# A hybrid trunk layer in split fp32: gate tiles spread over six delta heads, the attention branch moved beside the last two, state products in column strips

## Chip, cores and metric

The kernel runs on one core of one Trainium2 chip. The metric is device microseconds of one execution, here the median of three runs. Times inside the kernel come from one profiled execution, counted from its first instruction.

## What is computed

One layer of a decoder for 1024 prompt tokens and 8 single sample tokens (together NT = 1032 columns), width 1024. In short:

```
h   = RMSNorm(x) * (1 + scale1) + shift1
z   = h @ w_in            # q|k|v of the delta rule, its gate, beta, decay, q, k, v of attention, ga, gb
y_a = W_a( GatedRMSNorm( GatedDeltaRule( conv4(q, k, v) ) ) )
y_b = W_b( SlidingWindowSinkAttention(q, k, v) )
x   = x + gate1 * W_o( sigmoid(ga) * y_a + sigmoid(gb) * y_b )
x   = x + gate2 * W_down( silu(conv3(h2 @ W_gate)) * (h2 @ W_up) ),  h2 from x as h
```

The delta rule has 8 heads of 128 x 128 states. The prompt runs in eight chunks of 128 from a zero state. Each of the 8 samples has a carried state S per head and makes one step: S is scaled by exp(g), delta = (v - k S) * beta, then S + k delta, and q S is the output. All new states are outputs.

## The kernel before, in words

**Products.** Activations lie transposed: 128 channels in the partitions, tokens in columns, in eight channel blocks. Every fp32 operand is split into a high and a low half (`split`, L125: the high half on ScalarE, the difference on VectorE), and a product is three matmuls (`mm3`, L176). `project_steps` (L150) makes one output tile of 128 channels; the columns come in three *token parts* (`PARTS`: 384, 384 and 264 columns), each with 8 steps of 3 matmuls into one PSUM bank. A weight tile is 1024 x 128, 512 KB. `load_w` (L138) loads it on SyncE's DMA queue into a raw buffer and splits it into wh and wl. `where` names the pool: the main pool wp has two wh/wl pairs and one raw buffer, the side pool pg one of each.

**Order.** The order in the program isn't the order of issue. Each instruction has a priority from where the program stands (`cur_priority`), and a planner with a simulated timeline puts each engine's instructions in order: what is due first goes first, and what has a far priority goes where its engine would idle. `weave` (L1225) gives each stream of work a start and a step in that numbering; `issue_after` ties an instruction behind another. Once planned, each engine's order is fixed.

**Stages around the change.**

- Attention (up to about 435 us) leaves its output in DRAM (`ob`, 8 x 128 x 1032).
- Delta heads 0 to 7 (`run`, L1918). For each head h the streams are `unit_inverse` (L974, the inverse of a unit triangular 128 x 128 matrix from blocks of 16, 32 and 64), `delta_scan` (L910, eight chunks in sequence, each a chain of small matmuls with VectorE and ScalarE between), `delta_prepare` for head h+1, and `head_projections` (L791): for heads 0 to 5 the gate tile of head h (`delta_gate`, L834) and the three convolved tiles of head h+2. The output of a head goes to DRAM (`oa`).
- The filler. `gates` (L1248) is a generator of 16 weight tiles, sigmoid of gb and ga, stored to DRAM as `sgb` and `sga`. Each `next` is one step of three matmuls, 24 to a tile. Two tiles are drawn in the attention. Heads 0 to 5 draw `pieces(3)`, three parts, at a priority 10000 behind (L1927); the last two heads draw 12 and 24 pieces as `head_projections`, with loads in turn into side and main pool.
- Branches (`branches`, L1271). `ob` is loaded and split, for all three token parts, into rooms of its own. Then for each of 8 output tiles the weight `w_swa_out` is loaded once and multiplied with all three parts; the result times `sgb` stays in SBUF (`ub`). Between the parts stand the steps of `sample_delta` (L1095), the samples' delta rule, whose states and temporaries lie in the room of h (`b1`). Its products k S and q S (L1147) have a stationary operand of 16 columns and give 16 PSUM partitions. Its state stores go out on SyncE's queue, its output into the last 8 columns of `oa`. With the last two tiles `oa` is loaded and split. Then comes the product with `w_gdn_out`: times `sga`, plus `ub`, split into `mix`, which takes the room of `b1`.
- The second half (L1829): w_o, the second norm and the feed-forward part. The change doesn't touch it.

Names in profile lines: `b1h,wh` are products with h (projections and gate tiles), `b2h,wh` those of the branches; `rc`, `o` belong to the scan; `tp` to the inverse and preparation; `gt` is a gate tile's staging buffer; `raw` a raw weight buffer.

Of the kernel before, what the change touches and what calls it, by code (L numbers as in the profile page):

```python
# [9 lines left out]
F32 = mybir.dt.float32  # L10
# [8 lines left out]
P = 128  # L19
NP = 1024  # L20
NS = 8
# [41 lines left out]
class Step:  # L63
# [358 lines left out]
    def attention(self, pool, psum):  # L422
# [10 lines left out]
        self.filler, self.fill_where, self.gt = self.gates(), [self.where], (pool, "mrows")  # L433
# [298 lines left out]
    def delta_setup(self):  # L732
        nc = self.nc
        self.oa = self.t(self.dr, [8, P, NT], "oa")
# [43 lines left out]
    def delta_project(self, pa, pool, h):  # L778

        K = self.t(pool, [P, NCH, P], "K", bufs=3)  # L780
        Q = self.t(pool, [P, NCH, P], "Q", bufs=3)
        V = self.t(pool, [P, NCH, P], "v0", bufs=1)
# [51 lines left out]
    def delta_gate(self, pa, pool, h):  # L834

        nc = self.nc
        sg = self.t(pool, [P, NT], "sg", bufs=1)
# [9 lines left out]
        self.sg = sg  # L847
# [62 lines left out]
    def delta_scan(self, pool, psum, h, prep):  # L910
        nc, sg = self.nc, self.sg
# [183 lines left out]
    def sample_delta(self):  # L1095
# [3 lines left out]
        a, b, c, d, e = (self.t(self.b1, [P, KC, PARTS[t][1]], f"b1{x}{t}", F32R).bitcast(F32).rearrange("p k n -> p (k n)")  # L1099
                         for x, t in (("h", 1), ("l", 1), ("h", 2), ("l", 2), ("h", 0)))  # L1100
        small = carver(d, e)
        S0 = []
        for h in range(H):
            S0.append((a, b, c)[h // 3][:, h % 3 * NP:h % 3 * NP + NP].rearrange("p (b v) -> p b v", b=NS))
            nc.sync.dma_start(S0[h], I["state_gdn_S"][0][:, h].rearrange("b k v -> k b v"))
        act, tmp = small(24, NS), small(24, NS)
# [11 lines left out]
        wide = small(H, NS, 2 * NS)  # L1118
        nc.gpsimd.memset(wide, 0.0)
        yield  # L1120
        ps = self.t(self.psm, [P, 1], "mm")
# [12 lines left out]
        dots = self.t(self.psm, [P, H, NS], "mm")  # L1134
# [7 lines left out]
        rows = small(H, P, r=1)[:2 * NS]  # L1142
        for h0 in (0, 4):
            ps = self.t(self.psm, [2 * NS, 4, P], "mm")
            for h in range(4):
                for b in range(NS):
                    nc.tensor.matmul(ps[:, h, :], wide[:, h0 + h, b, :], S0[h0 + h][:, b, :], start=b == 0, stop=b == NS - 1)  # L1147
            nc.scalar.copy(rows[:, h0:h0 + 4, :], ps)
            yield
        pks = self.t(self.psm, [P, H, NS, 2], "mm")  # L1150
        for h in range(H):
            self.transpose(pks[:, h].rearrange("p b a -> p (b a)"), rows[:, h, :])
# [7 lines left out]
        ps = self.t(self.psm, [H * NS, P], "mm")  # L1160
        self.transpose(ps, f3(dl))
        dlT = small(P, r=1)[:H * NS]
# [9 lines left out]
        ps = self.t(self.psm, [H * NS, 1], "mm")  # L1172
# [5 lines left out]
        nc.vector.scalar_tensor_tensor(o, o, self.onw, self.sgs, op0=ALU.mult, op1=ALU.mult)  # L1178
        nc.sync.dma_start(self.oa[:, :, NP:NT].rearrange("i p b -> p i b"), o)

        for h in range(H):
            if h % 4 == 0:
                yield
            db = self.t(self.b1, [P, KC, 384], "b1l0", F32R).bitcast(F32).rearrange("p k n -> p (k n)") if h == 0 else db
            d = db[:, h % 3 * NP:h % 3 * NP + NP].rearrange("p (b v) -> p b v", b=NS)
            nc.sync.dma_start(d, dlr[h].unsqueeze(0).broadcast_to([P, NS, P]))
            nc.gpsimd.tensor_tensor(d, d, bc(kq[:, h, :, 0], 2, P), op=ALU.mult)
            for b in range(NS):
                nc.vector.scalar_tensor_tensor(S0[h][:, b, :], S0[h][:, b, :], self.egb[:, b, 0, h:h + 1], d[:, b, :],
                                               op0=ALU.mult, op1=ALU.add)  # L1190
            nc.sync.dma_start(self.O[3][0][:, h].rearrange("b k v -> k b v"), S0[h])

    def rows_rsqrt(self, small, ps, n, scale, eps):

        nc = self.nc
        r = small(2, r=1)
        nc.vector.tensor_scalar(r[:n, 0:1], ps, scale, eps, op0=ALU.mult, op1=ALU.add)
        self.power(r[:n, 1:2], r[:n, 0:1], self.mhalf)
        dg = small(P, r=1)
# [71 lines left out]
    def branches(self, pool, pool2):  # L1271
# [4 lines left out]
        for _ in self.filler:  # L1276
            pass
# [710 lines left out]
```

## Time and profile before

| what | value |
|---|---|
| median of 3 runs (lowest, highest) | 2168.84 us (2162.29, 2172.43) |
| the profiled execution | 2160.1 us, its span 2158.3 us |
| granted TensorE clock, mean | 0.976 |
| first state copy of the scans of heads 0 to 7 | 533, 616, 701, 779, 855, 930, 1007, 1093 us |
| last product with h (end of the gate tiles) | 1146.7 us |
| attention branch (`w_swa_out` products) | 1146.6 to about 1260 us |
| delta branch (`w_gdn_out` products) | about 1260 to 1350 us |

How to read the views: in the table of stages each row is a stretch, its length, then the busy time of each engine with its instructions in it, the granted TensorE clock (PEclk, 1.00 is full), the mean busy share of 16 DMA engines (it can go over 1, since overlapping packets are summed) and GB/s. PE is matmul, PEld weight load. A list of waits has who waited, for whom, the total, the number and the longest. A line of the timeline has start, duration, engine, line, operation, output and inputs, shape, count, and in brackets the idle time before it and what ended it. Matmuls are pipelined, so their durations overlap: what one costs is the distance between starts.

### The profile page before, as it was taken

Reading aid. Unit: us, or ns where it says so; the run is one execution under the profiler, and the core shown is the slowest. Engines: PE = TensorE matmul, PEld = TensorE weight load, DVE = VectorE, ACT = ScalarE, POOL = GpSimd, SP = SyncE. Lnnn points to the kernel's source line nnn. Section 1 sums busy time; section 2 is a strip of 40 time slices with the busy share of each in tenths; the row PEclk is TensorE's granted clock in tenths of the full one; section 3 lists DMA queues with packets and bytes.
Section 4 is the critical chain, followed back from the end, with each engine's and each line's share of the span. In section 5 each row is a group of like instructions: output and inputs, shape, how many; then the busy total and the mean of one; then the engine's idle time right before and its main releaser. Section 6 shows DMA issues by size and latency. Waiting matters only on the chain. (4 is left out here: it accounts for less than half of the span.)

```text
span 2158.3 us, 41369 instructions
## 1 busy us (share of the span) xinstructions
PE 2075.7 (96%) x16309; PEld 1957.4 (91%) x16309; DVE 1384.7 (64%) x2781; ACT 849.8 (39%) x2118; POOL 520.4 (24%) x583
## 2 busy tenths in 40 slices
PE   7999998999899999999999999999999999999998
PEld 4985887899899988998999999898999999999998
DVE  4756667374555756765323565468888788778876
ACT  3655446334234334344332032344333343444533
POOL 1000000020221110211111200002655655645631
PEclk8999999999999999999999999999999999999999
DMA  8256432151321321221318663612232323378962
GB/s 278 77 139 200 154 139 89 41 143 42 84 83 55 78 58 40 63 66 46 95 45 245 189 207 102 190 52 72 89 118 94 108 94 96 120 267 285 325 227 82
DMA packets 298981, 268.68 MB, mean 124 GB/s; under 512 B 60558, under 2 KB 246321, under 8 KB 298770
## 3 DMA queue, kind: packets, MB, share of 16 engines
q1 hardware_dynamic: 294450, 250.39, 37.3%
q0 software_dynamic: 4048, 15.12, 2.0%
q8 instruction: 128, 2.10, 0.4%
q14 instruction: 67, 0.55, 0.1%
q10 hardware_dynamic: 288, 0.52, 0.1%
HBM read 207.29 MB, written 61.07 MB: 124 GB/s over the span
## 5 line engine op out<-in xcount | busy, mean ns | idle before, releaser
L178 PE MATMUL mm<-b1h,wh 128*128 128x384 f32 (+1 forms) x1392 | 457.2, 329 | 4.5 <-ACT z L764 2.1
L180 PE MATMUL mm<-b1h,wl 128*128 128x384 f32 (+1 forms) x1392 | 452.2, 325 | 3.6 <-DVE wl L128 3.6
L179 PE MATMUL mm<-b1l,wh 128*128 128x384 f32 (+1 forms) x1392 | 450.0, 323 | 0.0
L178 PEld LDWEIGHTS mm<-b1h,wh 128*128 128x128 f32 x1392 | 263.6, 190 | 14.2 <-issue 4.7
L180 PEld LDWEIGHTS mm<-b1h,wl 128*128 128x128 f32 x1392 | 263.4, 189 | 10.1 <-issue 5.5
L179 PEld LDWEIGHTS mm<-b1l,wh 128*128 128x128 f32 x1392 | 263.6, 189 | 3.1 <-issue 2.8
L127 ACT ACTIVATE wh<-raw 128x1024 fp32r<-128x1024 f32 x75 | 78.7, 1049 | 158.3 <-PE mm L179 80.3
L128 DVE TENSOR_TENSOR wl<-raw,wh 128x1024 fp32r<-128x1024 f32 x74 | 90.7, 1225 | 66.5 <-ACT wh L127 65.8
L179 PE MATMUL mm<-pk,w 128*128 128x260 f32 (+1 forms) x440 | 124.9, 284 | 0.8 <-DVE pk L128 0.8
L178 PE MATMUL mm<-pk,w 128*128 128x260 f32 (+1 forms) x440 | 124.9, 284 | 0.6 <-ACT pk L127 0.6
L178 PE MATMUL mm<-b2h,wh 128*128 128x384 f32 (+1 forms) x384 | 123.4, 322 | 1.7 <-ACT wh L127 1.7
L180 PE MATMUL mm<-pk,w 128*128 128x260 f32 (+1 forms) x440 | 124.7, 284 | 0.0
L179 PE MATMUL mm<-b2l,wh 128*128 128x384 f32 (+1 forms) x384 | 122.7, 320 | 0.0
L180 PE MATMUL mm<-b2h,wl 128*128 128x384 f32 (+1 forms) x384 | 121.9, 320 | 0.6 <-DVE wl L128 0.6
L128 DVE TENSOR_TENSOR w<-ws,w 128x512 fp32r<-128x512 f32 x88 | 74.3, 846 | 37.7 <-ACT w L127 37.7
L1563 ACT COPY bml<-mm 128x256 f32<-128x256 f32 (+1 forms) x132 | 49.3, 374 | 107.7 <-PE mm L180 100.9
L178 PE MATMUL mm<-bmh,w 128*128 128x260 f32 (+1 forms) x320 | 90.7, 283 | 0.1
L180 PE MATMUL mm<-bmh,w 128*128 128x260 f32 (+1 forms) x320 | 90.5, 283 | 0.0
L179 PEld LDWEIGHTS mm<-pk,w 128*128 128x128 f32 x440 | 83.4, 189 | 1.0 <-DVE pk L128 1.0
L178 PEld LDWEIGHTS mm<-pk,w 128*128 128x128 f32 x440 | 83.4, 190 | 1.0 <-ACT pk L127 0.8
L180 PEld LDWEIGHTS mm<-pk,w 128*128 128x128 f32 x440 | 83.6, 190 | 0.0
L178 PEld LDWEIGHTS mm<-b2h,wh 128*128 128x128 f32 x384 | 72.7, 189 | 2.8 <-ACT wh L127 2.2
(632 smaller groups left out, 6081.5 us busy)
## 6 DMA issues: line engine op xcount, KB each, us to landing
raw<-in_w_in_dram SPq DMA_DIRECT2D x60, 512.0 KB
ws<-in_w_ffn_down_dram SPq DMA_DIRECT2D x55, 256.0 KB
raw<-xd SPq DMA_DIRECT2D x47, 258.0 KB
raw<-in_w_ffn_down_dram SPq DMA_DIRECT2D x47, 256.0 KB
raw<-in_w_ffn_gate_dram SPq DMA_DIRECT2D x22, 512.0 KB
raw<-in_w_ffn_up_dram SPq DMA_DIRECT2D x22, 512.0 KB
qst<-in_w_mod_dram SPq DMA_DIRECT2D x16, 512.0 KB
raw<-in_w_mod_dram SPq DMA_DIRECT2D x16, 512.0 KB
```

Of the source, the lines that this page charges most:

```text
L127: self.nc.scalar.activation(hi, x, AF.Copy)
L128: (eng or self.nc.vector).tensor_tensor(lo, x, hi.bitcast(F32), op=ALU.subtract)
L178: mm(ps, whi, xhi, start=first, stop=False, **kw)
L179: mm(ps, whi, xlo, start=False, stop=False, **kw)
L180: self.last_mm = mm(ps, wlo, xhi, start=False, stop=last, **kw).ins
L1563: self.last_copy = nc.scalar.copy(r[p, i], x[p])
```

## The change

- The delta heads 0 to 5 draw `pieces(6)` instead of 3: twice the gate parts.
- Head 6 draws both last delta gates (of heads 6 and 7), so `sg` is kept for each head; the second lies in a z buffer.
- A new generator `early_out` follows the gates in the filler: the attention branch, by token part (0, 2, 1), 24 parts of one output tile each. The weight tile is loaded anew for each part (two parts ahead; of three loads two go to the main pool and one to the side pool). `ob` goes into the rooms of h as these come free; the gated product goes to DRAM (`ubd`) and is read back in `branches`.
- The samples' chain runs in it: five steps early, the rest from the 17th part on. Its temporaries lie in the buffers K, Q, v0 and th of the delta heads (K, Q and v0 now in a pool of their own, pk), its PSUM tiles in `pmf`, a single buffer. The products k S and q S go to four strips of 32 PSUM partitions, four heads side by side, and eight transposes become two. State stores go out on GpSimd's queue. The samples' output stays in SBUF (`osm`).
- `branches` keeps only the delta branch; parts 0 and 1 of `oa` are given the priorities of the 18th and 21st part of the new filler. PSUM has a pool of four further buffers there instead of two and two.

The diff, cut to its core:

```diff
-        self.filler, self.fill_where, self.gt = self.gates(), [self.where], (pool, "mrows")
+        self.filler, self.fill_where, self.gt = chain(self.gates(), self.early_out()), [self.where], (pool, "mrows")
...
-        sg = self.t(pool, [P, NT], "sg", bufs=1)
+        sg = self.t(pool, [P, NT], "sg", bufs=1) if h + 1 < H else self.t(pa, [P, NT + 3], "z")[:, :NT]
...
+        e, f, g = (self.t(self.pk, [P, NCH, P], tag).rearrange("p n i -> p (n i)") for tag in ("K", "Q", "v0"))
+        small = carver(e, f, self.t(self.pa, [P, 512], "th"), g)
...
-        rows = small(H, P, r=1)[:2 * NS]
-        for h0 in (0, 4):
-            ps = self.t(self.psm, [2 * NS, 4, P], "mm")
+        rows = small(2, P, r=3)
+        nc.gpsimd.memset(rows, 0.0)
+        for i in range(2):
+            if i:
+                c, d = room("h", 2), room("l", 2)
+                for h in (6, 7):
+                    load(h, c)
+            ps = self.t(self.pmf, [P, P], "mm")
+            for b in range(NS):
+                for h in range(4):
+                    nc.tensor.matmul(ps[32 * h:32 * h + 2 * NS], wide[:, 4 * i + h, b, :], S0[4 * i + h][:, b, :],
+                                     start=b == 0, stop=b == NS - 1)
             for h in range(4):
-                for b in range(NS):
-                    nc.tensor.matmul(ps[:, h, :], wide[:, h0 + h, b, :], S0[h0 + h][:, b, :], start=b == 0, stop=b == NS - 1)
-            nc.scalar.copy(rows[:, h0:h0 + 4, :], ps)
+                at = slice(32 * h, 32 * h + 2 * NS)
+                (nc.scalar.copy if h % 2 else nc.vector.tensor_copy)(rows[at, i, :], ps[at])
             yield
...
-        nc.sync.dma_start(self.oa[:, :, NP:NT].rearrange("i p b -> p i b"), o)
...
-            nc.sync.dma_start(self.O[3][0][:, h].rearrange("b k v -> k b v"), S0[h])
+            nc.gpsimd.dma_start(self.O[3][0][:, h].rearrange("b k v -> k b v"), S0[h])
...
+    def early_out(self):
+        nc, order = self.nc, (0, 2, 1)
+        self.ubd = [self.t(self.dr, [8, P, n], f"ub{t}") for t, (_, n) in enumerate(PARTS)]
+        load = lambda i: self.load_w(self.I["w_swa_out"][0][:, i % 8 * P:(i % 8 + 1) * P],
+                                     where=self.fill_where[i % len(self.fill_where)])
+        X = {t: [self.part_room(self.b1, t, x, "b1") for x in "hl"] for t in (0, 2)}
+        self.load_part(self.ob, 0, *X[0])
+        samples = self.sample_delta()
+        ws, self.marks = [load(0), load(1)], []
...
+        g = gate(0)
+        for i in range(24):
+            t, j = order[i // 8], i % 8
+            self.marks.append(self.tc.cur_priority)
+            def out(t, ps):
+                nc.vector.tensor_tensor(s, ps, s, op=ALU.mult)
+                nc.sync.dma_start(self.ubd[t][j], s)
+            for k, _ in enumerate(self.project_steps(ws.pop(0), X, out, (t,), self.fill_psum)):
+                if k == 0:
+                    if i == 0:
+                        self.load_part(self.ob, 2, *X[2])
+                    if i == 8:
+                        X[1] = [self.part_room(self.b1, 0, x, "b1") for x in "hl"]
+                        self.load_part(self.ob, 1, *X[1])
+                    if i < 22:
+                        ws.append(load(i + 2))
+                    s, g = g, gate(i + 1) if i < 23 else None
+                if k in (2, 5) and (2 * i + k // 3 < 5 or i > 15):
+                    with self.tc.issue_after(self.last_mm):
+                        next(samples, None)
+                yield
...
-        ob = [self.load_part(pool2, self.ob, t) for t in range(3)]
+        here, oa = self.tc.cur_priority, []
+        for t, i in ((0, 17), (1, 20)):
+            self.tc.cur_priority = self.marks[i]
+            oa.append(self.load_part(self.oa, t, room[f"h{t}"], room[f"l{t}"]))
+        self.tc.cur_priority = here
+        oa.append(self.load_part(self.oa, 2, room["h2"], room["l2"], self.osm))
...
+        for t in range(3):
+            nc.sync.dma_start(ub[t], self.ubd[t].rearrange("j p n -> p j n"))
...
-        for j in range(6):
-            w = self.load_w(I["w_swa_out"][0][:, j * P:(j + 1) * P])
...
-                        self.fill_where, self.fill_psum = [self.fill_side, self.where], None
+                        self.fill_where, self.fill_psum = [self.where, self.fill_side, self.where], None
...
-                        streams.append((self.pieces(3), 10000, 100))
+                        streams.append((self.pieces(6), 10000, 100))
                     else:
-                        streams[1:1] = [(self.delta_gate(pa, pool, h), 500, 1)]
+                        if h + 2 == H:
+                            streams[1:1] = [(chain(*(self.delta_gate(pa, pool, i) for i in (h, h + 1))), 500, 1)]
                         streams.append((self.head_projections(pa, pool, h), 600, 100))
...
-            self.psm, more = self.pool("qs", 2, PSUM, ctx=c), self.pool("qb", 2, PSUM, ctx=c)
+            more = self.pool("qb", 4, PSUM, ctx=c)
```

111 lines of the change are left out of this document (54 added, 57 removed).

## The prediction, on record before the changed kernel ran

> **What bounds the kernel now.** First the head of the page, then the table of stages, with cuts at the first state copy of each delta head's scan (533, 616, 701, 1007, 1093), at the end of the gate tiles (1147) and at the start of the product of the delta branch (1260).
>
> ```profile
> span 2158.3 us, 41369 instructions
> PE 2075.7 (96%) x16309; PEld 1957.4 (91%) x16309; DVE 1384.7 (64%) x2781; ACT 849.8 (39%) x2118; POOL 520.4 (24%) x583
> ```
> ```profile
> core 0: us, PE busy (x) PEld busy (x) DVE busy (x) ACT busy (x) POOL busy (x), PEclk, DMA share, GB/s
> 533.00:616.00 83.00, 76.41 (x678) 72.22 (x677) 38.37 (x97) 29.12 (x96) 18.39 (x26) 0.96 0.28 78
> 616.00:701.00 85.00, 82.89 (x749) 79.97 (x747) 51.56 (x108) 30.70 (x85) 15.25 (x24) 1.00 0.24 64
> ...
> 701.00:1007.00 306.00, 288.91 (x2629) 275.64 (x2630) 197.89 (x438) 119.39 (x363) 47.20 (x74) 0.95 0.23 59
> ...
> 1007.00:1093.00 86.00, 84.38 (x749) 80.99 (x748) 32.86 (x93) 28.43 (x79) 16.35 (x24) 0.98 0.28 79
> 1093.00:1147.00 54.00, 53.97 (x363) 53.50 (x363) 14.96 (x29) 15.97 (x41) 10.22 (x15) 0.99 0.32 109
> 1147.00:1260.00 113.00, 109.28 (x723) 105.34 (x722) 57.26 (x132) 19.00 (x26) 21.30 (x13) 0.98 0.76 227
> 1260.00:1350.00 90.00, 89.71 (x574) 89.39 (x574) 52.08 (x108) 24.86 (x60) 0.00 (x0) 1.00 0.40 118
> ```
>
> TensorE bounds every stage, so moving a product gains nothing by itself; what can be gained is lost TensorE time. I count as lost the idle time (length minus PE busy) plus length times (1 minus PEclk). 701 to 1007: 17.1 idle + 306 x 0.05 = 15.3, together **32.4 us**. 616 to 701: 2.1. 533 to 616: 6.6 + 3.3 = 9.9. 1007 to 1147: 3.9. 1147 to 1260: 3.7 + 2.3 = **6.0**. After that nothing. Why the long stretch loses and the one before it doesn't, the stores of the gate tiles and the waits in that stretch say:
>
> ```profile
> L1263 SPq DMA_DIRECT2D sga<-gt x24: 319/320/1640, 1017.4 to 1165.2; - x24
> L1263 SPq DMA_DIRECT2D sgb<-gt x18: 319/335/580, 484.5 to 700.6; - x18
> L1263 SPq DMA_DIRECT2D sgb<-mrows x6: 319/320/320, 394.9 to 433.3; - x6
> ```
> ```profile
> PE tp L1058 <- ACT W L1049: 5.9, 4, 1.6
> PE rc L938 <- ACT s L936: 3.6, 7, 0.6
> PE rc L934 <- DVE y L932: 2.2, 4, 1.6
> PE rc L188 <- DVE vn L960: 2.1, 3, 0.7
> ```
>
> A gate tile is three parts, so three stores. Two tiles lie in the attention (x6), six (x18) between 484 and 701, eight (x24) from 1017. The filler of six heads is used up in the first three: from 701 to 1007 TensorE waits in the chain of the block inverse and the scan with nothing put between.
>
> **The change, part by part.** A tile of 8 x 3 parts x 3 products takes 90 / 8 = 11.25 us (row 1260: 8 tiles); by columns 4.2 us for a part of 384 and 2.9 us for the one of 264.
>
> *Twice the filler in six heads.* Six tiles, 67.5 us, leave the stretch behind 1007 and come ahead of it: no work gained or lost. The gain is lost time filled. The streams of 701 to 1007 are those of 616 to 701, where five parts brought the loss to 2.1; over 306 us at that rate it is 2.1 x 306/85 = 7.6, so 32.4 - 7.6 = **-24.8**. Supply: five parts in 85 us are 18 parts, six tiles, in 306 us, just what is added. The other end is 533 to 616, where four tiles stood with no projections and 9.9 was lost: 9.9 x 306/83 = 36.5, a loss of 4. I take -24.8, since the nearest row has the same streams.
>
> *Products with the sample states.*
>
> ```profile
> L1147 PE MATMUL mm<-b1h,b1l x80: 272/273/282, 1169.9 to 1188.2; 128*16 128x128 f32 x80
> L1147 PE MATMUL mm<-b1l,b1l x48: 272/273/282, 1175.1 to 1184.7; 128*16 128x128 f32 x48
> ```
> ```profile
> 175.61 1.07 PE L262 MATMUL mm<-wmh,cTr 128*32 128x512 f32 x2 [0.56 <-DMA wmh<-in_w_mod_dram]
> 175.62 1.07 PE L262 MATMUL mm<-wml,cTr 128*32 128x512 f32 x2
> 176.47 1.07 PE L262 MATMUL mm<-wmh,cTr 128*32 128x512 f32 x2
> ```
>
> 128 records between 1169.9 and 1188.5; a 4.4 us product tile lies between, so 14.3 us, 0.11 each. In four column strips four run side by side, as the modulation's do, whose starts in one group lie 0.01 us apart: 14.3 / 4 = 3.6, **-10.7**. Bounds: nothing (weight loads that don't overlap) and -10.7; the modulation is the only row of such strips, and it overlaps. Eight transposes become two; the eight small copies lie on ACT and DVE, which idle.
>
> *The attention branch as filler.* Its 24 parts (90 us) and the samples' chain move beside the last two heads, whose filler was the gates: cover is the same in kind, so their 3.9 stays, and the branch stage's 6.0 goes: **-6.0**. New is supply. The old order loaded a 512 KB weight tile for three parts, the new one for each part: 16 loads more, and 16 splits more on ACT (1.06) and DVE (1.22), 17 and 20 us that lie in idle time of both (row 1007). Two loads of three go through the one raw buffer of the main weight pool, which comes free after the DVE split:
>
> ```profile
> 1173.02 0.38 SPq L133 DMA_DIRECT2D raw<-in_w_swa_out_dram  x1
> ...
> 1179.61 0.38 SPq L133 DMA_DIRECT2D raw<-in_w_swa_out_dram  x1
> ```
> ```profile
> 1177.26 1.06 ACT L127 ACTIVATE wh<-raw 128x1024 fp32r<-128x1024 f32 x1 [5.64 <-DMA raw<-in_w_swa_out_dram]
> ```
> ```profile
> 1178.36 1.23 DVE L128 TENSOR_TENSOR wl<-raw,wh 128x1024 fp32r<-128x1024 f32 x1 [4.55 <-ACT wh L127]
> ```
> ```profile
> 1217.05 1.06 SPq L133 DMA_DIRECT2D raw<-in_w_swa_out_dram  x1
> ```
> ```profile
> 1224.29 1.06 ACT L127 ACTIVATE wh<-raw 128x1024 fp32r<-128x1024 f32 x1 [15.40 <-DMA raw<-in_w_swa_out_dram]
> ```
>
> From issue to issue one cycle is 6.6 us when DMA is quiet, and 7.2 + 1.1 + 1.2 = 9.5 when it isn't. Three parts need two cycles: 13.2 to 19. The parts of token part 0 lie beside the scan, which covers them. Token part 2 takes 8.7 per three: 4.5 short, 9 us over the six parts that come after the scan. Token part 1 takes 12.6: 0.6 to 6.4 short, 2 to 17 us over eight parts. Sum 11 to 26; I take 15, near the quiet cycle. Change from gate tiles to this filler: the rooms of h part 0 are refilled from DRAM, and TensorE has only the last tile's other two parts (7.1 us):
>
> ```profile
> L1217 SPq DMA_DIRECT2D b2l<-ob x12: 360/447/1361, 1136.7 to 1146.1; - x12
> ```
> ```profile
> 1145.07 0.85 ACT L127 ACTIVATE b2h<-b2l 128x768 fp32r<-128x768 f32 x1 [0.21 <-DMA b2l<-ob]
> ```
>
> First issue to fourth split was 1136.7 to 1145.9, 9.2 us, so 2 are left. Together **+17**.
>
> *Queues.* SP issues 16 loads, 24 stores of the gated products and 3 reads more, and 8 state stores and one of the samples' output less: 34 x 0.38 = 13 us over some 200 us; nothing, while SP doesn't wait. The state stores move to GpSimd's queue, behind its eight products per state; nobody waits there. Samples' temporaries now take the single spare PSUM buffer, which every third product tile also takes: nothing while evacuations keep pace, up to 5 if each of some ten steps makes a tile wait half a microsecond. The reads of the last token part come when two parts of the next product have run; seven PSUM buffers cover them.
>
> **Sum** against the profiled execution (span 2158.3, 2160.1 with what lies around it): -24.8 - 10.7 - 6.0 + 17 = **-24.5**, so 2136. The median shown is 2168.84, 8.7 above that execution; carried over, **2144**.
>
> **Rivals.** (a) *The loads are hidden*: the planner puts state steps and scan between, and the 17 is 0: -41.5, 2127. For it: DMA share is 0.28 and 0.32 in the last two heads; against: the single raw buffer.
>
> (b) *The gain is eaten*: -10 to +10, 2168. Either the filler is again used up early, in four heads instead of six (half of -24.8), with loads at 9.5; or stalls reach 40. For it: six heads' filler was gone after three.
>
> (c) *Slower: the attention branch becomes bound by DMA.* Its stretch moves 12.6 MB of weights, 4.2 each of attention output, states read, states stored, broadcast deltas, gates and gated products, and 6.2 of early reads for the next stage: 44 MB, in about 105 us of TensorE work (90 of parts, the rest scan and samples).
>
> ```profile
> 1210.00:1262.00 52.00, 47.99 (x291) 46.55 (x290) 38.32 (x89) 9.52 (x11) 14.38 (x8) 0.97 0.85 264
> ...
> 1146.00:1170.00 24.00, 24.00 (x159) 23.85 (x158) 11.97 (x26) 7.08 (x12) 5.50 (x4) 1.00 1.13 314
> 1218.00:1260.00 42.00, 38.92 (x237) 38.01 (x238) 28.32 (x75) 7.63 (x9) 10.22 (x5) 0.96 1.00 310
> ```
>
> At the 264 GB/s of the first row 44 MB take 167 us, +62 instead of +17: +20, **2189**. It decides below 300 GB/s (147 us, +42, which eats -41.5), if all 44 MB must land before the next stage. For it: the three rows are that traffic at a full DMA. Against: stores and early reads (10 MB) needn't land in it, and the other 34 MB take 110 us at 310.
>
> The Trainium skill speaks on this in "DMA: Bandwidth & Descriptors", section Specifications: HBM gives one core about 358 GB/s. By that limit the 44 MB would take 123 us, an estimate, +18, and (c) couldn't be slower. The rows saturate at 310 to 314 with 512-byte runs, so I don't lower its chance for it.
>
> The skill's page "TensorE: Matmul & The Clock Gate", section "Why this matters for your kernels", says the clock drops for TensorE idle gaps over about 3 us. The longest wait of the rows above is 1.6 us and yet PEclk is 0.95 in that stretch. By the rule filling would return idle time alone, 17.1 - 7.6 = 9.5 instead of 24.8, and the time would be 2160: it falls into (b), and as the rows speak against it I add nothing there.
>
> **How the numbers follow.** Forecast (2134 to 2157) 0.42, (a) 0.20, (b) 0.15, (c) 0.23. Faster by over 0.5% (10.8 us, about what a measurement of this kernel can tell from no change) is forecast and (a): 0.62; within: 0.15; slower: 0.23. The range goes from full filling without stalls (-49 with all of 32.4 returned, 2120) to (c): 2118 to 2188.
>
> **What would show it.** Right: gate stores spread to about 1000, PEclk 0.98 or more between 701 and the sixth head, the state products in about 4 us, first product of the delta branch some 20 us earlier, and TensorE waits of 10 to 20 us in all on the DVE split of weights or on a loaded weight. Wrong: gate stores that stop before 900; waits on weights over 40 us; DMA share at 1 over all of the branch; waits on GpSimd or the single PSUM buffer.

## The result, and the profile after

The changed kernel takes **2179.17 us** in the median (2174.00 to 2183.69 in 11 runs), the kernel before on the same chips 2169.91 (2162.07 to 2176.66 in 11): a ratio of **1.0044**, 95% interval 1.0026 to 1.0062, so 9.5 us slower by the ratio and 9.3 between the medians. 2144 was forecast; the range of 2118 to 2188 holds the time, the sign is wrong. All ratios use fast runs alone; the only slow one, 3399.34 us in the experiment on the operand reads, is left out.

The profiled execution has a span of 2172.3 us. Its table of stages is cut at the first state copies of the scans and, behind 1054, where the waits change:

```profile
700.00:788.00 88.00, 86.64 (x768) 84.10 (x767) 51.13 (x111) 32.10 (x97) 14.99 (x23) 1.00 0.27 71
788.00:882.00 94.00, 92.03 (x801) 90.12 (x802) 53.24 (x118) 35.85 (x111) 17.50 (x26) 0.98 0.26 68
882.00:967.00 85.00, 83.32 (x750) 80.36 (x749) 50.64 (x105) 30.49 (x84) 14.84 (x24) 1.00 0.24 64
967.00:1054.00 87.00, 82.87 (x748) 80.69 (x747) 53.89 (x118) 32.86 (x100) 14.20 (x21) 0.98 0.28 73
1054.00:1108.00 54.00, 52.29 (x466) 50.41 (x464) 30.56 (x85) 17.86 (x54) 11.59 (x18) 1.00 0.42 113
1108.00:1151.00 43.00, 37.72 (x342) 33.51 (x340) 18.64 (x36) 16.83 (x29) 2.31 (x3) 0.94 0.77 228
1151.00:1180.00 29.00, 25.17 (x161) 23.98 (x159) 14.21 (x27) 10.60 (x23) 1.59 (x1) 0.91 0.53 162
1180.00:1207.00 27.00, 24.79 (x185) 23.70 (x185) 12.99 (x22) 8.01 (x16) 2.40 (x3) 1.00 0.65 185
1207.00:1265.00 58.00, 43.20 (x266) 38.62 (x267) 32.38 (x69) 15.07 (x18) 12.59 (x10) 0.88 0.84 253
1265.00:1286.00 21.00, 19.52 (x110) 19.11 (x109) 10.16 (x24) 3.67 (x6) 5.41 (x4) 0.92 1.05 357
1286.00:1355.00 69.00, 68.04 (x441) 67.44 (x439) 47.67 (x117) 18.09 (x51) 5.74 (x4) 1.00 0.53 159
```

Lost time is counted as in the prediction, idle time plus length times (1 minus PEclk). The scans of heads 2 to 5 (700 to 1054) lose 12.8 us now, where 32.4 were lost. The scan of head 6 begins at 1053.6 instead of 1007.5, and this execution had begun its heads 2.8 earlier: 67.5 us of filler came in for 48.9, a gain of **18.6**. Behind it, 1054 to 1355, **44.2 us** are lost: 1.7, 7.9, 6.4, 2.2, 21.8, 3.2 and 1.0 row by row. Before, it was 3.9 + 6.0 + 0.3 = 10.2 from 1007 to 1350. The change put one hole in the place of another.

The ledger by first state copies, last evacuation of the delta branch (1350.4 before, 1354.5 after) and first product with w_o (1352.5, 1362.8):

| stretch | before | after | forecast | measured |
|---|---|---|---|---|
| to the first scan | 532.6 | 529.8 | 0 | -2.8 |
| scans 0 to 5, with 67.5 us more filler | 474.9 | 523.8 | -24.8 | -18.6 |
| from scan 6 to the last delta evacuation, with 67.5 less | 342.9 | 300.9 | +0.3 (-10.7 - 6.0 + 17) | +25.5 |
| to the first w_o product | 2.1 | 8.3 | 0 | +6.2 |
| from there to the end | 805.8 | 809.5 | 0 | +3.7 |
| span | 2158.3 | 2172.3 | -24.5 | +14.0 |

The gate stores show that the filler reaches as far as it was meant to: six of them, two tiles, lie behind the start of scan 6, and the last is at 1115. The products with the states run in two halves, the first from 1129.2 to 1131.1; of the second two start at 1216.0, and after a further wait for a state the rest runs from 1218.2 to 1221.4:

```profile
L1280 SPq DMA_DIRECT2D sga<-gt x24: 319/332/1703, 704.3 to 1115.2; - x24
```
```profile
L1157 PE MATMUL mm<-b1h,Q x80: 272/273/421, 1129.2 to 1221.2; 128*16 128x128 f32 x80
...
L1157 PE MATMUL mm<-b1l,Q x48: 272/385/421, 1129.2 to 1221.0; 128*16 128x128 f32 x48
```

The waits of TensorE from 1054 to 1365 (total, times, longest), then those of SyncE's queue from 1100 to 1290:

```profile
PE mm L1418 <- ACT w L127: 8.3, 1, 8.3
PE mm L180 <- DVE wl L128: 7.4, 8, 3.9
PE mm L178 <- ACT wh L127: 6.6, 8, 1.4
PE mm L1157 <- DMA b1h<-in_state_gdn_S_dram: 5.9, 2, 4.3
PE rc L934 <- DVE y L932: 2.3, 2, 1.5
PE mm L188 <- ACT th L1090: 2.0, 1, 2.0
```
```profile
SPq L1302 <- DMA ub<-gt: 24.5, 12, 5.7
SPq L1312 <- DVE gt L1311: 15.6, 10, 4.2
SPq L133 <- DVE wl L128: 7.2, 6, 2.4
```

TensorE waits 14.0 us for weight tiles, 5.9 for the states of heads 6 and 7, 8.3 for w_o. All the waits of that window, the short ones that are not shown too, come to 37.7 us, and the rows above add some 14 us of lowered clock from 1108 to 1286. SyncE's queue, which issues nearly every load, stands still for 113 us of 190: gate reads wait until a product store has left their buffer, stores wait for their product, and the loads of weights, states and operands stand behind them. That alone shows no cause, though: in the same 190 us of the kernel before, the queue stood still for 124, and TensorE lost little.

At w_o the order had turned round. SyncE's queue after, then before:

```profile
1348.95 7.53 SPq L1410 DMA_DIRECT2D x<-xT  x16
1356.58 3.76 SPq L1427 DMA_DIRECT2D raw<-in_w_o_dram  x3
```
```profile
1342.09 2.60 SPq L1383 DMA_DIRECT2D raw<-in_w_o_dram  x3
1350.38 1.76 SPq L1366 DMA_DIRECT2D x<-xT  x4
```

The second half's raw buffers lie at a fixed place on the left of SBUF. Since the two pools of the branches changed places and part 2's operand lies in the one that is now first, this place was the operand of token part 2, the last one used, instead of that of part 0.

### The profile page after: what moved, and what is told of

It is laid out like the page before. It is cut to its first block, busy times and chain, and to the rows that moved or that the text cites. A ratio compares the mean times of both kernels' runs of the same rounds, so it can differ in the third digit from the quotient of the medians.

```text
span 2172.3 us, 41439 instructions
## 1 busy us (share of the span) xinstructions
PE 2062.6 (95%) x16303; PEld 1941.5 (89%) x16303; DVE 1404.1 (65%) x2802; ACT 863.2 (40%) x2137; POOL 530.0 (24%) x592
## 5 line engine op out<-in xcount | busy, mean ns | idle before, releaser
L178 PE MATMUL mm<-b1h,wh 128*128 128x384 f32 (+1 forms) x1584 | 521.8, 331 | 10.6 <-ACT wh L127 4.7
L180 PE MATMUL mm<-b1h,wl 128*128 128x384 f32 (+1 forms) x1584 | 515.6, 326 | 6.4 <-DVE wl L128 6.4
L179 PE MATMUL mm<-b1l,wh 128*128 128x384 f32 (+1 forms) x1584 | 512.6, 324 | 0.1
L178 PEld LDWEIGHTS mm<-b1h,wh 128*128 128x128 f32 x1584 | 300.0, 190 | 23.2 <-ACT wh L127 6.1
L180 PEld LDWEIGHTS mm<-b1h,wl 128*128 128x128 f32 x1584 | 299.8, 189 | 14.9 <-DVE wl L128 8.5
L179 PEld LDWEIGHTS mm<-b1l,wh 128*128 128x128 f32 x1584 | 300.4, 190 | 3.3 <-issue 2.8
L127 ACT ACTIVATE w<-ws 128x512 fp32r<-128x512 f32 x88 | 55.4, 632 | 49.3 <-PE wv L180 45.0
L1279 POOL TENSOR_SCALAR gt<-gt 128x384 f32<-128x384 f32 (+1 forms) x42 | 30.4, 724 | 180.1 <-ACT gt L1278 180.1
L179 PE MATMUL mm<-bmh,w 128*128 128x256 f32 (+1 forms) x264 | 74.2, 281 | 0.0
L128 DVE TENSOR_TENSOR w<-raw,w 128x512 fp32r<-128x512 f32 (+1 forms) x69 | 61.7, 895 | 18.3 <-ACT w L127 18.1
```

The source lines that it names most:

```text
L127: self.nc.scalar.activation(hi, x, AF.Copy)
L128: (eng or self.nc.vector).tensor_tensor(lo, x, hi.bitcast(F32), op=ALU.subtract)
L178: mm(ps, whi, xhi, start=first, stop=False, **kw)
L179: mm(ps, whi, xlo, start=False, stop=False, **kw)
L180: self.last_mm = mm(ps, wlo, xhi, start=False, stop=last, **kw).ins
L1279: nc.gpsimd.tensor_scalar(s, s, 0.5, 0.5, op0=ALU.mult, op1=ALU.add)
```

## The experiments

Theory A: the reloaded weights, through their few raw buffers (called the ring below), are the new loss. B: DMA's throughput. C and D: the order of SyncE's one queue (C the gate reads and product stores in it, D the early reads of the delta branch's operand). Beside them stand the late states, the room of w_o, and the two good parts alone. Each ratio is to the kernel before, with its interval; differences in us are worked out from the ratios unless medians are named. Half an interval is 3 to 5 us, so a difference between two experiments under some 5 us is not resolved.

**The filler alone.**

```diff
-                        streams.append((self.pieces(3), 10000, 100))
+                        streams.append((self.pieces(5), 10000, 100))
...
-            yield from self.pieces(24 if h + 1 == H else 12)
+            yield from self.pieces(24 if h + 1 == H else 6)
```

> The kernel before with one number changed: heads 0 to 5 draw five parts of gate tiles each instead of three, and head 6 draws six, so that four tiles (45 us of products) move from the last two heads into the stretch from 701 to 1007 us. Nothing else of the change is in it. In the changed kernel 67.5 us of filler came in for 48.8 us of time, so 0.28 of it fell into lost time. Theory (filling is a gain of its own): 0.28 x 45 = -12.5 us, ratio 0.994. Rival (what is taken from the last two heads is missed there as much): they lose as head 3 to 5 did, 32.4 us in 306, so 0.11 us per us over some 95 us = +10, and the ratio is 0.999 to 1.000.

Measured: **1.0040** [1.0023, 1.0058], +8.7 us. 702 to 789 is full now. Three later stages, then the longest wait from 1037 to 1165:

```profile
1037.00:1106.00 69.00, 64.09 (x603) 60.59 (x603) 30.49 (x90) 23.60 (x71) 11.63 (x18) 0.92 0.22 61
1106.00:1147.00 41.00, 31.83 (x217) 31.15 (x215) 11.21 (x29) 9.14 (x31) 7.78 (x11) 0.87 0.43 113
1147.00:1165.00 18.00, 9.59 (x44) 9.19 (x45) 9.25 (x11) 9.03 (x12) 0.00 (x0) 0.66 1.09 358
```
```profile
PE mm L178 <- ACT b2h L127: 12.4, 1, 12.4
```

The scan of head 6 begins at 1037.4 instead of 1007.5: 45 us of filler for 29.9, 15 gained. From 1037 on 39.4 us are lost (10.4, 14.5, 14.5): the last two heads have too little, and no gate tile is left to cover the load of the attention branch's operand. The rival was right in kind and too small. Moving the gates to earlier heads alone gains nothing; the change needed new filler behind it.

**The strips alone.**

```diff
-        for h0 in (0, 4):
-            ps = self.t(self.psm, [2 * NS, 4, P], "mm")
...
+            ps = self.t(self.psm, [P, P], "mm")
+            for b in range(NS):
+                for h in range(4):
+                    nc.tensor.matmul(ps[32 * h:32 * h + 2 * NS], wide[:, 4 * i + h, b, :], S0[4 * i + h][:, b, :],
+                                     start=b == 0, stop=b == NS - 1)
```

> The kernel before with the products of the sample states alone in four column strips, and two transposes for eight. Theory (they cost path time, as the prediction has it): 128 products in 3.6 us instead of 14.3, -10.7 us, ratio 0.995. In the changed kernel's trace two halves of 64 took 1.8 and 3.1 us. Rival (the planner had them beside waits, or the eight narrow copies hold up what follows): 0 to -4 us, ratio 0.998 to 1.000.

Measured: **0.9944** [0.9923, 0.9965], -12.1 us by the ratio and -10.8 between the medians (2158.21 and 2169.0). The -10.7 was right within the interval, and this is the fastest kernel of the study. Both together, with one gate part more per head:

> The kernel before with the column strips and with four gate parts per head instead of three for heads 0 to 5: two tiles (22.5 us) leave the last two heads. Strips alone gave 0.9944; five parts alone gave 1.004. Theory (filler taken from the last two heads is missed there more than it gains): half of the +7 of five parts or less, +0 to +4 us against the strips alone, ratio 0.9945 to 0.9965. Rival (the last two heads can spare two tiles, only not four): 0.28 x 22.5 = -6 us, 0.9915.

0.9965 [0.9950, 0.9980], 4.6 us above the strips alone: the upper end of what the theory had, though the two intervals overlap. The rival's 0.9915 lies outside the interval, so moving two tiles did not gain either.

**The late states.** Two `yield` between the loads of the states of heads 6 and 7 and the second half of the products.

> The changed kernel, with two steps of the samples' chain (about 4 us of products) put between the loads of the states of heads 6 and 7 and their products. In the changed kernel TensorE waits 5.9 us for these two loads, in a stretch with a granted clock of 0.88. Theory (the late loads are a cause of the loss): the 5.9 us go, and with the clock 2 to 4 us more, so -6 to -10 us against the changed kernel: ratio to the kernel before 1.000 to 1.002 instead of 1.0044. Rival (the stretch is short of loaded weights, and a wait removed here comes back on the next weight tile): no change, 1.004, with waits on L127 and L128 grown by 4 to 6 us.

1.0071 [1.0051, 1.0092], no better than the changed kernel. The wait stays:

```profile
PE mm L1159 <- DMA b1h<-in_state_gdn_S_dram: 6.3, 2, 4.7
```

The edit did not move them apart: the loads were issued at 1212.7 and 1215.2, behind operand reads and a product store in SyncE's queue. The products of that half started at 1215.2, and those with the late states waited until 1220.7 and 1222.9. What these states cost by themselves is left open.

**The room of w_o.** In turn: the last pair of output tiles in the order 2, 0, 1; that and x on GpSimd's queue for the first quarter; the order 2, 1, 0.

```diff
-            for t in range(3):
+            for t in (2, 1, 0) if j0 else range(3):
                 for j in (j0, j0 + 1):
                     self.project(w[j - j0], oa, ya_out, (t,))
```

> The changed kernel, with one line of the delta branch changed: the last pair of output tiles takes the token parts in the order 2, 0, 1 instead of 0, 1, 2. The room into which w_o is loaded lies, since the two pools of the branch changed places, over the operand of part 2, where it lay over that of part 0 before. Theory (this room is what makes the first product with w_o wait 8.3 us instead of 2.1): the load goes out some 10 us earlier, the wait falls to about 2, -6 us against the changed kernel, ratio 1.0015 to 1.002. Rival (the load is late because SyncE's queue holds the reads of x ahead of it, or since DMA is busy with stores): the wait stays at 6 to 8 us, ratio 1.004.

> The changed kernel, with part 2 ahead of parts 0 and 1 in the last pair of output tiles of the delta branch, and the reads of x for the first quarter of w_o on GpSimd's queue. With the first edit alone TensorE waited 9.2 us for w_o: SyncE's queue had six reads of x ahead of w_o, which waited from 1346.3 to 1356.3 for the room that part 1's operand holds. Theory (room and queue order together make the wait): both are gone now, w_o is issued some 12 us earlier, the wait falls from 8.3 to 2 us or less, -6 us against the changed kernel, ratio 1.0015 to 1.002. Rival (the wait is in the DMA or in the splits of the new weights): it stays above 6, 1.0045.

> The changed kernel, with the token parts of the last pair of output tiles of the delta branch in the order 2, 1, 0. The room of w_o's raw buffers lies over part 2's operand, that of x over part 1's, so both come free before the last product now, and nothing in SyncE's queue has to wait for the last part. Theory (rooms under the last part, with an in-order queue in front, make the wait of 8.3 us): w_o is issued by 1352 or before, the wait falls to about 2, -6 us against the changed kernel, ratio 1.0015 to 1.003. Rival: the first product now waits for part 0's last results to be gated and split, some 2 to 4 us, and the gain is 2 to 4, ratio 1.0025 to 1.0035.

1.0055 [1.0037, 1.0073], 1.0063 [1.0047, 1.0080] and 1.0035 [1.0019, 1.0052]. The waits for w_o are 9.2, 11.0 and 2.4 us. SyncE's queue with 2, 0, 1, then with 2, 1, 0:

```profile
1356.35 2.69 SPq L1410 DMA_DIRECT2D x<-xT  x6
1359.09 3.80 SPq L1427 DMA_DIRECT2D raw<-in_w_o_dram  x3
```
```profile
1349.58 2.69 SPq L1410 DMA_DIRECT2D x<-xT  x6
1352.31 2.87 SPq L1427 DMA_DIRECT2D raw<-in_w_o_dram  x3
```
```profile
PE mm L1418 <- ACT w L127: 2.4, 1, 2.4
```

With the first, w_o's room was free early, but six reads of x stood ahead of it, whose room lies over part 1's operand. Sending the first quarter's reads elsewhere left those of the later quarters in front. Only when both rooms come free before the last part does w_o go out in time. The mechanism is shown, 5.9 us of wait; of these 2 came back alone, which the intervals don't resolve, and 5 together with the next edit.

**Fewer reloads.** Parts 0 and 2 of an output tile share a weight tile (16 loads for 24); then that with the order 2, 1, 0:

```diff
+        order = [(t, j) for j in range(6) for t in (0, 2)] + [(0, 6), (0, 7), (2, 6), (2, 7)] + [(1, j) for j in range(8)]
```

> The changed kernel, with the 24 parts of the attention branch in another order: token parts 0 and 2 of an output tile one behind the other with one weight tile, then part 1. 16 weight loads instead of 24, 4.2 MB less through DMA, 8 splits fewer, 8 entries fewer in SyncE's queue. Theory A (weights reloaded for each part are what the branch is short of): of the 14 us of TensorE waits on their splits half goes, and with the clock -6 to -10 us against the changed kernel, ratio to the kernel before 1.000 to 1.002. Theory B (DMA as such is the limit, at some 264 GB/s): 4.2 MB are 16 us, ratio 0.997. Theory C (the limit is the order of SyncE's queue, in which loads wait behind the gate reads and product stores): 0 to -5 us, 1.002 to 1.0045.

> The changed kernel with both edits that were made alone: 16 weight loads for 24 (-3.9 us against the changed kernel) and the order 2, 1, 0 in the delta branch's last pair. Theory (two separate waits): the sum, -8 to -10, ratio 0.9995 to 1.001. Rival (the first only moves when DMA is full, so that what it saves is lost again at w_o): as the first alone, 1.0026.

1.0026 [1.0011, 1.0042] and 1.0003 [0.9988, 1.0019]: 3.9 (not resolved) and 8.9 us better than the changed kernel. The first does not bear out A: the ratio lies in C's range (its interval reaches into A's), and TensorE's waits for weight tiles did not halve (15.3 us, where 14.0 were). The second came out at the sum that was expected, though the two edits alone gave 3.9 and 2.0. And no reload at all:

> The changed kernel, where only the first eight weight tiles of the attention branch are loaded and the other 16 parts use the eighth one again, so the attention branch's output is left without its right weights for token parts 1 and 2. 16 loads, 8.4 MB and 16 splits go. An upper bound for everything that the reloading costs. Theory A: all 14 us of waits on weight splits go, and most of the lost clock of 1151 to 1265 (about 10 us): -14 to -24 us against the changed kernel, ratio 0.993 to 0.998. Theory B (DMA as such): 8.4 MB at 264 GB/s are 32 us of DMA, TensorE becomes the bound again, -25 us, 0.993. Theory C (SyncE's queue held up by gate reads and product stores): the waits on weights go, but those on states, samples and operands stay or grow, -5 to -12, 0.999 to 1.002.

0.9977 [0.9963, 0.9990], **14.5 us** better than the changed kernel. Its first waits from 1100 to 1370, then four of its stages:

```profile
PE mm L1420 <- ACT w L127: 7.8, 1, 7.8
PE mm L178 <- DVE gt L1311: 4.5, 1, 4.5
PE mm L1219 <- DVE gt L1311: 1.8, 2, 1.1
PE mm L178 <- ACT wh L127: 1.7, 2, 1.0
```
```profile
1107.00:1150.00 43.00, 38.80 (x339) 34.46 (x338) 18.10 (x35) 16.66 (x29) 1.91 (x3) 0.89 0.74 221
1150.00:1180.00 30.00, 28.52 (x198) 28.05 (x198) 13.08 (x28) 8.21 (x21) 1.01 (x1) 0.93 0.36 112
...
1203.00:1250.00 47.00, 42.18 (x290) 40.16 (x289) 20.96 (x63) 2.47 (x5) 13.68 (x10) 1.00 0.62 197
1250.00:1272.00 22.00, 18.62 (x89) 17.80 (x90) 10.89 (x27) 3.58 (x5) 7.79 (x6) 0.77 0.98 352
```

The waits for weights are all but gone (2.2 us) and those for the states too; the gain is A's lower bound. Loads, bytes, splits and places in the queue all went at once, so this does not tell A from B and C. But the prediction without its reload term of 15 would have been -39.5, and this kernel is 5 us faster than the one before: the distance to the forecast is 34 us without the reloads as with them. They were costed rightly, and what went wrong is something else: these four rows lose 8.9, 3.6, 4.8 and 8.4 us, and from 1052 to 1272 it is 28.3 in all, with no weight reloaded.

**The queue, the ring, the traffic.** Gate reads and product stores moved to GpSimd's queue; the weights in halves through the same raw buffer; all of it with the pairs.

```diff
-            nc.sync.dma_start(s, self.sgb[i % 8][:, lo:lo + n])
+            nc.gpsimd.dma_start(s, self.sgb[i % 8][:, lo:lo + n])
...
-                nc.sync.dma_start(self.ubd[t][j], s)
+                nc.gpsimd.dma_start(self.ubd[t][j], s)
```
```diff
+            for k in (slice(0, 4), slice(4, 8)):
+                nc.sync.dma_start(raw[:, k], src[:, k])
+                self.split(hi[:, k], lo[:, k], raw[:, k], self.lo_engine)
```

> The changed kernel, with the reads of the gates and the stores of the gated products of the attention branch on GpSimd's DMA queue instead of SyncE's: two words changed. Bytes, loads and order otherwise the same. From 1100 to 1290 SyncE's queue waits some 110 us in all, 24.5 of them for the landing of a product store before the next gate read, 15.6 for the product before its store, and the loads of weights, states and operands stand behind. Theory C (the order of that queue is the limit): TensorE's waits on weight splits (14 us) and on the states of heads 6 and 7 (5.9) fall to a third, and with the clock -12 to -22 us against the changed kernel, ratio 0.994 to 0.999. Theory A (one raw buffer for two of three weight tiles) and theory B (DMA's throughput): the same bytes through the same buffers, 0 to -3 us, 1.003 to 1.0045; or worse, if GpSimd's own work is held up behind its queue.

> The changed kernel, with each weight tile of the attention branch loaded in two halves of 256 KB and split half by half, in the same raw buffer: the load of one half can run while the other is split and used. Bytes the same, 24 DMAs and 48 splits more. With gate reads and stores out of SyncE's queue its loads still waited 26.9 us for the splits and 22.3 for the last raw load. Theory A (the ring of the one raw buffer is the supply): the waits on weight splits (14 us) fall by half, -5 to -10 us, ratio 1.000 to 1.002. Theory B (DMA's throughput and latency under load, whatever the buffer): no gain, 1.0035 to 1.006, the additional DMAs and splits costing 0 to 3 us.

> The changed kernel with the pairs (16 loads), the half loads and the order 2, 1, 0 together. If all three are separate causes: -4, -5 to -10 and -6, so 0.996 to 0.999. If DMA's throughput is what is left after the pairs: 1.000 to 1.001 as with the pairs and the order alone. In no case is the whole loss of the branch (forecast 26 below what was measured) back: the changeover to the branch, from 1108 to 1180, isn't touched.

> The kernel with pairs and the order 2, 1, 0 (1.0003), with the gate reads and the product stores of the attention branch on GpSimd's queue. With all 24 loads this was +8.7 us against the changed kernel, the loads waiting for their ring of raw buffers instead. Theory C (queue order, once the ring has slack): the 5.9 + 2.6 us of waits on a gate read's product and part of the 13 us on weight splits go, -4 to -8, 0.9965 to 0.9985. Rival (transfers on GpSimd's queue come later, and the state updates that GpSimd works on stand behind them): +4 to +9 as before, 1.002 to 1.0045.

1.0084 [1.0067, 1.0101], 1.0030 [1.0016, 1.0043], 1.0023 [1.0009, 1.0038] and 1.0020 [0.9998, 1.0042]. With the gates out of its queue, SyncE waited for the ring instead:

```profile
SPq L133 <- DVE wl L128: 26.9, 11, 5.8
SPq L133 <- DMA raw<-in_w_swa_out_dram: 22.3, 7, 5.9
```

So C falls as a remedy: what SyncE no longer waited for gates it waited for the ring, and the move cost 8.7 us, with the pairs 3.7 (not resolved). Whether the transfers come later on GpSimd's queue was not separated from that. The halves cut the waits for weights from 14.0 to 6.0 us and the time by 3 (not resolved); with the pairs and 2, 1, 0 they gained nothing. Then 6.3 MB less behind the last head, where the kernel leaves out the new states of heads 2 to 7:

```diff
+            if h < 2:
                 nc.sync.dma_start(u, dlr[h].unsqueeze(0).broadcast_to([P, NS, P]))
...
+            if h < 2:
                 nc.gpsimd.dma_start(self.O[3][0][:, h].rearrange("b k v -> k b v"), S0[h])
```

> The changed kernel, where the broadcast reads of the samples' deltas and the stores of the samples' new states are made for heads 0 and 1 only, so the new states of heads 2 to 7 are left out: 12 DMAs of 512 KB, 6.3 MB, less between 1236 and 1296 us. No product of TensorE waits for any of them. From 1180 to 1286 the changed kernel moves 27.2 MB at 256 GB/s. Theory B (behind the last head DMA's throughput is the bound): 6.3 MB at 256 to 357 GB/s are 18 to 25 us of DMA; about half of these transfers lie before the delta branch has its operands, so -8 to -15 us, ratio 0.9975 to 1.001. Theory C (chain of the samples and order of the queues): 0 to -4 us, 1.0025 to 1.0045, since the chain's steps and SyncE's waits for products and stores stay.

> The same omission (new states of samples for heads 2 to 7 left out, 6.3 MB) in the kernel with pairs and the order 2, 1, 0, which alone gave 1.0003. Theory B: DMA at 365 GB/s from 1240 to 1265 and 6.5 us of wait for a w_gdn_out tile there; -8 to -15 us, ratio 0.9935 to 0.9965. Theory C: 0 to -4 us, 0.9985 to 1.0003.

1.0035 [1.0019, 1.0051] and 1.0003 [0.9989, 1.0018]: 2 us and none, both within noise, and both outside B's ranges. B falls in the form I gave it: transfers that no product waits for take little from those that one waits for, though DMA is full in part of the stretch.

**The order of the early operand reads.** In the kernel with pairs and 2, 1, 0, parts 0 and 1 of `oa` are tied behind the fifteenth and sixteenth weight load; in the changed kernel behind the last two of 24.

```diff
+            with self.tc.issue_after(self.w_loads[14 + t]):
+                oa.append(self.load_part(self.oa, t, room[f"h{t}"], room[f"l{t}"]))
```

> The kernel with pairs and the order 2, 1, 0 (1.0003), where the early reads of the delta branch's operand are tied behind the loads of the last two weight tiles but one and the last of the attention branch: part 0 behind the fifteenth load, part 1 behind the sixteenth. Same bytes, same buffers. Theory D (the weights stand behind these reads, in the queue and on a full DMA): the waits of 5.9, 2.6, 5.0 us and the lost clock of 1180 to 1240 shrink, -6 to -12 us, 0.995 to 0.9975, if the reads, some 10 us of DMA at 310 GB/s, still land before the delta branch begins. Rival (the same reads then make the delta branch wait): the waits move to its first operands, -2 to +4 us, 0.9995 to 1.002.

> The changed kernel with one edit: the early reads of the delta branch's operand are tied behind the loads of the last weight tiles but one (part 0) and the last (part 1) of the attention branch; in SyncE's queue three weight loads still come behind part 0's reads. Theory D (the order of these reads is a cause of its own): -5 to -8 us against the changed kernel, ratio 1.0005 to 1.002. Rival (with 24 loads the ring of raw buffers is the limit there, whatever stands in the queue): 0 to -2 us, 1.0035 to 1.0045.

**0.9971** [0.9952, 0.9991] against 1.0003, and **1.0093** [1.0071, 1.0115] against 1.0044. The kernel with pairs and 2, 1, 0, then the same with the reads tied:

```profile
1108.00:1142.00 34.00, 30.73 (x334) 27.39 (x332) 12.67 (x29) 13.91 (x27) 0.00 (x0) 1.00 0.66 198
1142.00:1180.00 38.00, 38.00 (x272) 37.97 (x271) 15.38 (x35) 8.61 (x27) 2.83 (x3) 1.00 0.42 126
1180.00:1205.00 25.00, 19.14 (x142) 18.52 (x144) 15.32 (x18) 12.74 (x15) 0.57 (x1) 0.96 1.05 328
1205.00:1240.00 35.00, 24.79 (x140) 23.11 (x130) 17.67 (x42) 5.14 (x8) 7.59 (x6) 0.79 0.62 186
1240.00:1265.00 25.00, 17.65 (x104) 16.91 (x104) 13.28 (x34) 4.42 (x6) 6.89 (x6) 0.91 1.04 365
```
```profile
1180.00:1207.00 27.00, 23.83 (x205) 23.02 (x203) 10.06 (x13) 7.00 (x8) 0.57 (x1) 0.98 0.86 250
1207.00:1240.00 33.00, 27.24 (x127) 25.09 (x127) 21.44 (x43) 12.61 (x19) 5.21 (x4) 0.86 0.79 257
1240.00:1265.00 25.00, 15.77 (x80) 14.62 (x81) 13.91 (x32) 2.38 (x3) 7.64 (x7) 0.84 1.00 341
```

Lost time from 1180 to 1240 falls from 24.5 to 14.1 (5.9 + 1.0 + 10.2 + 7.4; 3.2 + 0.5 + 5.8 + 4.6), and the next row loses 3.6 more. In the kernel with all 24 loads the same edit made it worse: TensorE waited 13.8 us for the high halves of weights, one wait of 6.6 for a w_gdn_out tile at 1283, and 1265 to 1300 lost 11.5 us, where the changed kernel loses 3.7 there:

```profile
PE mm L178 <- ACT wh L127: 13.8, 7, 6.6
```
```profile
1265.00:1300.00 35.00, 28.39 (x156) 27.93 (x155) 18.49 (x49) 6.50 (x14) 7.52 (x6) 0.86 0.89 306
```

D holds with 16 loads and fails with 24. The parts of the shortfall don't add up; this edit to the queue's order paid only where 8 loads fewer went through it.

## Why the prediction was right or wrong

- **What bounds the kernel, and the hole in the scans of heads 2 to 5: right.** Filling them brought 18.6 of the 24.8. The rate of the neighbouring stretch (2.1 in 85) was better than what came, 12.8 in 354 us. With that the clock came back too: 0.95 to between 0.98 and 1.00, although the waits there had never been longer than 1.6 us. The Trainium skill, "TensorE: Matmul & The Clock Gate", section "Why this matters for your kernels", has the clock drop for gaps over about 3 us; by it only 9.5 would have returned. The rows decide against it here.
- **Strips: right**, -10.7 against 10.8 (medians) and 12.1 (ratio) measured alone. In the changed kernel a wait of 5.9 for two late states stands beside them, which was not foreseen.
- **The reloads, +15 of the +17: right in size.** Without them 14.5 us come back. The sum behind it is short at its upper end: token part 2 was taken at the quiet cycle alone, and at 19 for three it would be 20.6 short instead of 9, so 11 to 38 instead of 11 to 26.
- **The step that failed: "cover is the same in kind, so their 3.9 stays, and the branch stage's 6.0 goes".** Lost time behind the start of scan 6 was to go from 10.2 to about 21. It went to 44.2, and none of the 23 between was in the sum. Beside the last two scans (1054 to 1207) 18.2 us are lost, where 3.9 and 2 for the changeover were allowed; behind them (1207 to 1355) 26.0, where 15.3 were. The reloads don't explain it: with none at all, 28.3 us are lost from 1052 to 1272, where the prediction without its 15 had about 6.
- **"Queues ... nothing, while SP doesn't wait" failed too, in its condition.** The queue already stood still for 124 of the 190 us from 1100 to 1290 in the kernel before, and does for 113 in the changed one; so standing still doesn't show the cause. That its order counts the edits show: one moved the time by -6.9 us in one kernel and by +10.6 in another. The loads had been judged one by one, each against TensorE's time, but not the one queue and the few buffers that they share in the order that the planner fixes. How much of the 23 each of them makes is not settled (below).
- **The changeover** was costed at 2. From 1108 to 1180, 14.3 us are lost; with two parts for each weight tile 3.3 (1108 to 1142 lost 3.3 us of 34, the row from 1142 nothing). That speaks against the refilled room of h as the cause. It is not shown that supply of weights is: of 8.2 us of waits from 1100 to 1180 only 1.1 end with a weight tile, the others with results of the scan, the inverse and the samples, and without any reload 12.5 are still lost there.
- **w_o, +6.2: not foreseen.** The swap of two pools was in the diff, and the prediction has no term for it. It moved the room of the next stage's first load under the last operand in use.
- **Rival (c)** had the sign, with 2189, and its traffic: 44.9 MB moved from 1100 to 1290, at 236 GB/s, below the 300 at which it was to decide. But 6.3 MB less changed the time by 2 us at most, so the mean rate was not DMA's limit. The fullest rows reached 357, 358 and 365 GB/s, so the 310 to 314 that the prediction took for saturation was not the ceiling. The Trainium skill, "DMA: Bandwidth & Descriptors", section Specifications, gives about 358 GB/s for a core; these rows come out near it. A row of the kernel before could have said as much, 60 us at 349 GB/s in the second half:

```profile
1920.00:1980.00 60.00, 60.00 (x505) 60.00 (x504) 43.78 (x53) 25.59 (x36) 31.20 (x21) 1.00 0.96 349
```

- **Rival (b)** had the size, -10 to +10, and neither of its reasons: the filler lasted, and the waits for the ring were 14, not 40.

**What stays open**: between the forecast of -24.5 and the +14.0 of the profiled executions lie 38.5 us: 6.2 in the filler, 6.2 at w_o, 0.9 at both ends, and 25.2 between the scan of head 6 and the end of the delta branch. Those no single edit gave back: 6.3 MB less gained 2 us at most, another queue lost, half loads gained 3 (not resolved), another order of the operand reads gained or lost. The late states were not parted from the queue, and no version was tried in which all of the branch's loads go in a better order, nor one with other filler beside the last two scans. The 3.7 us in the second half and the 2.8 at the start are not explained.

## What to carry to other kernels

When work is moved under other work, count what it needs per unit of time through each *shared* thing on its way, the queue and the raw buffer as well as bytes; "off the path" holds for one load, not for forty in a fixed order. Hold a wait that you find afterwards against the same stretch of the kernel before, where the queue may have waited as long. Filler moved from a place that needs it is worth nothing: the sum of holes has to shrink, and the small edit that shortened work by itself (the strips alone, 0.9944) was the only part shown to pay in full. Read a swap of two allocations like a change of schedule: ask which later load lands on the operand used last.

## What the runs showed of the hardware

- Fp32 products of 16 columns by 128 in four column strips ran at four times the rate of single ones: 64 in 1.8 us against 128 in 14.3. Where the granted clock was 0.57 (1218.2 to 1221.4), the last 62 of 64 took 3.2.
- The granted clock fell without long waits: 0.94 from 1108 to 1151, where the longest wait is 2.0 us. The lower clock makes 13.8 of the 41.5 us lost between 1108 and 1286.
- One core's DMA moved 357 to 365 GB/s for 18 to 25 us at a time, and 349 for 60 us in the kernel before.
